# Five arriving-weight slots and nine split-weight slots become four and ten, with a table and four decay rows rehoused

## The chip, the core and the metric

The kernel runs on one core of a Trainium2 chip. The metric is the device time of one execution in microseconds (us): 879.27 us is the median of three runs of the kernel before (878.99 to 879.74).

## What is computed

Two transformer blocks of depth 2 and 1 are run after one another on a sequence of 256 tokens of width 1024, all in fp32. Cut to what matters:

```
for i in range(2):                                   # first_block
    h = x @ w_in[i]
    mix = gated spatial mixer (i = 0)  or  12-head causal attention (i = 1)
    mem_out = 4-head attention of q_mem into 256 memory tokens
    x = layer_norm(ALPHA * x + concat(mix, mem_out) @ w_mix_out[i])
    x = layer_norm(ALPHA * x + (silu(x @ w_g) * (x @ w_u)) @ w_ffn_out[i])     # FFN A, FFN B
mod = silu(c) @ w_ada + b_ada                        # second_block: six rows of 1024
h = rms_norm(x) * (1 + scale1) + shift1
mix = concat(short convolution, 4-head retention with rotary q and k and decay rows) @ w_out
x = x + gate1 * rms_norm(mix)
h = rms_norm(x) * (1 + scale2) + shift2
x = x + gate2 * rms_norm(relu(h @ w_fc1)**2 @ w_fc2)                           # FFN D
```

## The kernel before, in words

**Weights.** All projection weights come from one packed tensor, `w_packed`, in 512 KB pieces (128 partitions by 1024 fp32). A piece is fetched by one DMA of the SP queue into a `raw` slot (L219). Then `split` makes two fp32r tiles of it in an `hl` slot: ScalarE casts the high part (L199), and VectorE subtracts that from `raw` to get the low part (L200). The raw slot is free when the subtraction ends. The hl slot is free when the last matmul that reads it ends. A product then takes three matmuls: high by high, low by high and high by low (`mm_s`, L261; `mm_w2`, L279 and L284; `mm_w`, L269).

**Order.** `weight_plan` lists the chunks in the order of use; an entry has one to four pieces. `chunk(key)` fetches ahead to the entry that is at least LEAD = 6 pieces past the one in use. The tile framework fixes, when the program is built, one order for each engine, by the order of the program, the raised priority of some stretches (`urgent`) and its own estimate of when slots come free; at run time every queue keeps that order. A boundary (`close`, `open_units`) is a layer norm between two stages.

**The slots.** `BUFS` gives five raw and nine hl slots. In the gated FFNs (A and B, 11 pairs of 256 columns) an iteration of the loop over p takes a "g" entry of four pieces (L279 and L284, from both halves of the gate) and an "o" entry of two pieces (L261), for the output of pair p - 2.

**The adaLN rows.** `ada_step` computes `silu(c) @ w_ada` on VectorE (L777, L779) from w_ada pieces of 512 KB, which are loaded into the same raw slots (L774): 32 pieces in FFN A, four after each of the pairs p = 2 to 9, and 16 in FFN B, two after each of p = 2 to 7 and four after p = 8. `ada_end` multiplies the sums with ones on TensorE (L788).

**The small tiles.** `sm(shape, tag)` has a number of slots for each tag, from `SMALL`, otherwise four. The tag `qm` has one slot of 128 by 512 fp32. It holds the memory queries of each layer, and in the retention the decay rows of one head after another (`dec`, L973, loaded at L974 and read at L981). `tab` holds the cosine and sine of the rotary embedding; `rotary_tables` fills it during FFN B (L865 to L885), and `qk_proj` reads it (L967, L968).

Of the kernel before, what the change touches and what calls it, by code (L numbers as in the profile page):

```python
# [10 lines left out]
F32 = mybir.dt.float32  # L11
# [7 lines left out]
P = 128  # L19
S = 256  # L20
D = 1024
# [6 lines left out]
SMALL = {'cg': 2, 'hs': 2, 'sg': 2, 'up': 2, 'qm': 1, 'pr': 4, 'pt': 2}  # L28
LEAD = 6
NS = {'A': 2, 'B': 2, 'D': 4}  # L30
BUFS = {'raw': 5, 'hl': 9, 'ph': 8, 'bc': 4}
FINE = 2
LAG = {'A': 1, 'B': 1, 'D': 2}
WARM = 10
# [98 lines left out]
def model_kernel(  # L133
# [10 lines left out]
    const = ctx.enter_context(tc.tile_pool(name="const", bufs=1))  # L144
    rawp = ctx.enter_context(tc.tile_pool(name="rawp", bufs=BUFS["raw"]))
    hlp = ctx.enter_context(tc.tile_pool(name="hlp", bufs=BUFS["hl"]))
    actp = ctx.enter_context(tc.tile_pool(name="actp", bufs=2))
    bcp = ctx.enter_context(tc.tile_pool(name="bcp", bufs=BUFS["bc"]))
    php = ctx.enter_context(tc.tile_pool(name="php", bufs=BUFS["ph"]))
    smp = ctx.enter_context(tc.tile_pool(name="smp", bufs=2))  # L150
# [5 lines left out]
    def nm(s):  # L156
        uid[0] += 1
        return f"{s}{uid[0]}"

    def bank():  # L160
        return psp.tile([P, 512], F32, tag="ps", name=nm("ps"))
# [2 lines left out]
        return php.tile(shape, dt, tag="ph", name=nm("ph"))  # L164

    def sm(shape, tag, dt=F32):
        return smp.tile(shape, dt, tag=tag, name=nm(tag), bufs=SMALL.get(tag, 4))


    ident = const.tile([P, P], F32, name="ident")  # L170
# [56 lines left out]
    def chunk(key):  # L227
        state["at"] = at_of[key]
        fetch(ahead())
        return ready[key]  # L230


    def urgent():
        return tc.high_priority(offset=URGENT)
# [52 lines left out]
    def joined(dst, o):  # L287

        c = sm([P, S], "cg")
        nc.scalar.copy(c, o[:, S:])  # L290
        return nc.vector.tensor_add(dst, o[:, :S], c)  # L291

    def rstd_of(v0, v1, eps):

        r = sm([P, 1], "rstd")
        nc.vector.tensor_scalar(r, v0, v1, eps, op0=OP.add, op1=OP.add)  # L296
        nc.gpsimd.tensor_tensor(r, r, mhalf, op=OP.pow)  # L297
        return r
# [16 lines left out]
    def layer_norm_act(t, accs, g, b):  # L315

        xx = xt[t]
        s = sm([P, 2], "st")
        for h, cs in enumerate(HALVES):
            nc.vector.scalar_tensor_tensor(xx[:, cs], xx[:, cs], ALPHA, accs[h], op0=OP.mult, op1=OP.add,  # L320
                                           accum_out=s[:, h:h + 1])
        nb = sm([P, 1], "nb")
        nc.vector.tensor_scalar(nb, s[:, 0:1], s[:, 1:2], -1.0 / (32.0 * D), op0=OP.add, op1=OP.mult)
        v = sm([P, 2], "mv")
        junk = bank()
        for h, cs in enumerate(HALVES):
            nc.scalar.activation(junk, xx[:, cs], AF.Square, bias=nb, scale=1.0 / 32.0, accum_out=v[:, h:h + 1])
        nmu = sm([P, 1], "nmu")
        nc.vector.tensor_scalar(nmu, nb, 32.0, None, op0=OP.mult)
        for cs in HALVES:  # L330
            nc.vector.scalar_tensor_tensor(xx[:, cs], xx[:, cs], nmu, g[:, cs], op0=OP.add, op1=OP.mult)
        r = rstd_of(v[:, 0:1], v[:, 1:2], LN_EPS)
        for cs in HALVES:
            nc.vector.scalar_tensor_tensor(xx[:, cs], xx[:, cs], r, b[:, cs], op0=OP.mult, op1=OP.add)
# [324 lines left out]
            nc.vector.bn_stats(st3[t][:, b], vl[t][:, S * b:S * b + S])  # L659

    def v_norm(t):
        mv = sm([P, 2], "mv2")
        nc.vector.bn_aggr(mv, st3[t])
        r = rstd_of(mv[:, 1:2], 0.0, LN_EPS)
        nc.vector.scalar_tensor_tensor(vl[t], vl[t], mv[:, 0:1], lvg, op0=OP.subtract, op1=OP.mult)
        nc.vector.scalar_tensor_tensor(vl[t], vl[t], r, lvb, op0=OP.mult, op1=OP.add)
# [15 lines left out]
    hl = chunk(("Av", 0))  # L682
# [12 lines left out]
    for h in range(2):  # L695
        nc.sync.dma_start(bsb[64 * h:64 * h + 64], bass.AP(
            tensor=a_b_s.tensor, offset=a_b_s.offset + P * h, ap=[[0, 64], [2 * P, 6], [1, P]]))
    v_norm(0)
    v_norm(1)
    ubuf = [ph([P, 3, S]) for _ in range(2)]  # L700
    for j in range(6):
# [30 lines left out]
    qm = sm([P, 2, S], "qm")  # L732
# [94 lines left out]
    qm = sm([P, 2, S], "qm")  # L827
# [28 lines left out]
    close([part(0, 3)], [part(1, 2), part(1, 3)], mixo.acc, bnd)  # L856


    tab = const.tile([P, 2, S], F32, name="tab")
    freq = const.tile([P, 2], F32, name="freq")  # L860

    def rotary_tables():
# [107 lines left out]

    def ret_scores(h):

        dec = sm([P, 384], "qm")  # L973
        nc.sync.dma_start(dec, k_decay[h])  # L974
        q, k = qk_of[h][:, 0], qk_of[h][:, 1]
        ps = bank()
        nc.tensor.matmul(ps[:, :S], k[:, :P], q, start=True, stop=True)
        nc.tensor.matmul(ps[:, S:384], k[:, P:], q[:, P:], start=True, stop=True)
        s_of[h] = sm([P, 384], "pt")
        with urgent():  # L980
            nc.vector.tensor_mul(s_of[h], ps[:, :384], dec)  # L981
# [61 lines left out]
    for h in range(4):  # L1043
        qk_proj(h, 0)
        if h >= 2:
            ret_scores(h - 2)
        qk_proj(h, 1)
        if h >= 2:
            ret_values(h - 2)
    y = conv_in(0)  # L1050
    ret_scores(2)
    conv_out(0, y)
    ret_values(2)
    ret_scores(3)
    y = conv_in(1)
    ret_values(3)
# [105 lines left out]
```

## Time and profile before

| | |
|---|---|
| median of three runs | 879.27 us |
| the profiled execution | 880.1 us, of which its span is 876.9 us |
| TensorE matmul busy | 866.3 us, 99% of the span |
| TensorE weight load busy | 730.0 us, 83% |
| VectorE, ScalarE busy | 650.3 us (74%), 488.1 us (56%) |
| moved by DMA | 195.7 MB, mean 223 GB/s |

The difference of 3.2 us between the execution and its span lies outside the profile's instructions. Matmuls overlap one another in the profile, so the busy share of TensorE shows that it was never left without work for long, not that each matmul ran at its shortest.

### The profile page before, as it was taken

To read this page: it belongs to the slowest core of one execution; us is meant where nothing else is said; L and a number is where in the kernel's file an instruction comes from. 1 tells how busy PE (TensorE), PEld (TensorE's weight loads), DVE (VectorE), ACT (ScalarE), POOL (GpSimd) and SP (SyncE) were. 2 spreads that over 40 slices of the span, in tenths; PEclk is the share of its full clock that TensorE was granted. 3 is DMA by queue.
4 is the path that set the end of the run, shared out by engine and by line. 5 is a ranking of instruction groups with operands and counts; after the bars stand their busy time and mean duration, and the time that the engine had idled before them with its cause. 6 is when DMAs were issued, how large, how long until landed. Compare 5 with 4: busy or idle time off the path is not lost.

```text
span 876.9 us, 12811 instructions
## 1 busy us (share of the span) xinstructions
PE 866.3 (99%) x4678; PEld 730.0 (83%) x4678; DVE 650.3 (74%) x982; ACT 488.1 (56%) x887; POOL 21.5 (2%) x32
## 2 busy tenths in 40 slices
PE   9999999999999999999999999999999999999997
PEld 6888888888887888778888888878988888888885
DVE  6877967888989778767877767797777975555542
ACT  6666454545544567545645644565555676666641
POOL 0100000000000000000000000020010100000000
PEclk9999999999999999999999999999999999999999
DMA  8987757888987763426876777558645566555511
GB/s 317 329 287 228 239 188 253 287 302 308 317 297 258 240 240 121 144 93 200 306 245 230 246 264 266 206 181 290 210 168 195 180 212 213 191 192 191 188 56 48
DMA packets 60355, 195.70 MB, mean 223 GB/s; under 512 B 9209, under 2 KB 12537, under 8 KB 60293
## 3 DMA queue, kind: packets, MB, share of 16 engines
q1 hardware_dynamic: 59860, 194.57, 65.5%
q8 instruction: 36, 0.59, 0.3%
q10 hardware_dynamic: 432, 0.33, 0.1%
q14 instruction: 27, 0.21, 0.1%
HBM read 193.80 MB, written 1.07 MB: 222 GB/s over the span
## 4 chain that ended last, share of the span: by engine, by line
PE 82%; DVE 6%; DMA 5%; issue 3%; ACT 3%; POOL 0%; SPq 0%; POOLq 0%; DVEq 0%; ACTq 0%
PE ps L261 38%; PE ps L279 23%; PE ps L284 12%; DMA raw<-w_ada 4%; DVE hl L200 3%; PE ps L269 3%; ACT hl L199 2%; DMA raw<-w_packed 1%; PE ps L590 1%; PE ps L547 1%; DVE ph L779 1%; PE ps L686 1%; PE ps L244 1%; PE ps L581 1%; POOL rstd L297 0%
## 5 line engine op out<-in xcount | busy, mean ns | idle before, releaser
L200 DVE TENSOR_TENSOR hl<-raw,hl 128x1024 fp32r<-128x1024 f32 (+1 forms) x294 | 348.2, 1204 | 112.7 <-ACT hl L199 112.0
L199 ACT CAST hl<-raw 128x1024 fp32r<-128x1024 f32 (+1 forms) x294 | 296.8, 1039 | 133.3 <-DMA raw<-w_packed 58.0
L261 PE MATMUL ps<-hl,ph 128*128 128x512 f32 x912 | 213.0, 390 | 0.0
L261 PEld LDWEIGHTS ps<-hl,ph 128*128 128x128 f32 x912 | 171.0, 188 | 36.2 <-ACT cg L290 0.8
L279 PE MATMUL ps<-yT,hl 128*128 128x512 f32 x576 | 147.6, 393 | 0.0
L279 PEld LDWEIGHTS ps<-yT,hl 128*128 128x128 f32 x576 | 104.5, 189 | 19.5 <-issue 0.8
L284 PEld LDWEIGHTS ps<-yT,hl 128*128 128x128 f32 x576 | 78.6, 190 | 5.9 <-DVE hl L200 0.3
L284 PE MATMUL ps<-yT,hl 128*128 128x256 f32 x576 | 80.6, 282 | 0.1
L290 ACT COPY cg<-ps 128x256 f32<-128x256 f32 x134 | 48.9, 367 | 51.5 <-PE ps L279 51.3
L261 PE MATMUL ps<-hl,mixT 128*128 128x512 f32 x288 | 70.0, 396 | 0.0
L779 DVE SCALAR_TENSOR_TENSOR ph<-raw,cT,ph 128x1024 f32<-128x1024 f32 x42 | 53.8, 1282 | 19.0 <-DMA raw<-w_ada 18.3
L261 PEld LDWEIGHTS ps<-hl,mixT 128*128 128x128 f32 x288 | 53.0, 188 | 12.9 <-issue 2.2
L279 PE MATMUL ps<-fT,hl 128*128 128x512 f32 x192 | 50.2, 392 | 0.0
L279 PE MATMUL ps<-xT,hl 128*128 128x512 f32 x176 | 46.9, 397 | 0.0
L199 ACT CAST ph<-hs 128x256 fp32r<-128x256 f32 x60 | 24.4, 406 | 38.6 <-DVE hs L452 37.8
L261 PE MATMUL ps<-hl,yT 128*128 128x512 f32 x192 | 45.3, 392 | 0.1
L261 PEld LDWEIGHTS ps<-hl,yT 128*128 128x128 f32 x192 | 35.6, 188 | 8.3 <-ACT yT L249 0.5
L200 DVE TENSOR_TENSOR ph<-hs,ph 128x256 fp32r<-128x256 f32 x60 | 25.3, 422 | 21.4 <-ACT ph L199 20.1
L279 PEld LDWEIGHTS ps<-fT,hl 128*128 128x128 f32 x192 | 35.2, 189 | 6.3
L279 PEld LDWEIGHTS ps<-xT,hl 128*128 128x128 f32 x176 | 31.6, 189 | 6.8 <-issue 1.0
L297 POOL TENSOR_TENSOR rstd<-rstd,mhalf 128x1 f32<-128x1 f32 x18 | 17.1, 949 | 788.8 <-DVE rstd L296 788.8
L450 ACT ACTIVATE sg<-sg 128x256 f32<-128x256 f32 x36 | 15.0, 418 | 30.6 <-DVE sg L291 30.6
(181 smaller groups left out, 932.2 us busy)
## 6 DMA issues: line engine op xcount, KB each, us to landing
raw<-w_packed SPq DMA_DIRECT2D x286, 512.0 KB
raw<-w_ada SPq DMA_DIRECT2D x48, 512.0 KB
bc<-mod SPq DMA_DIRECT2D x6, 512.0 KB
raw<-w_packed SPq DMA_DIRECT2D x8, 256.0 KB
ph<-x_t SPq DMA_DIRECT2D x8, 128.0 KB
ph<-mem_t SPq DMA_DIRECT2D x2, 512.0 KB
xt<-x SPq DMA_DIRECT2D x2, 512.0 KB
bc<-ln_mix_g SPq DMA_DIRECT2D x2, 512.0 KB
```

The lines of the kernel that those rows point to most:

```text
L199: a = nc.scalar.copy(dst_hi, src)
L200: b = nc.vector.tensor_sub(dst_lo, src, dst_hi.bitcast(F32))
L244: nc.tensor.transpose(p4[:, k], src[:, 512 * h + P * k:512 * h + P * (k + 1)], ident)
L261: nc.tensor.matmul(o, aT[:, a, k0 + k, tok], hl(b, k, cols), start=start and n == 0, stop=stop and n == 3 * nk - 1)
L269: nc.tensor.matmul(o, hl(b, k, cols), aT[:, a, k, :], start=n == 0, stop=n == 3 * nk - 1)
L279: nc.tensor.matmul(both, hl(0, k, cols), aT[:, :, k, :], start=k == 0, stop=k == nk - 1)
L284: nc.tensor.matmul(o[:, :S], hl(1, k, cols), aT[:, 0, k, :], start=False, stop=False)
L290: nc.scalar.copy(c, o[:, S:])
L297: nc.gpsimd.tensor_tensor(r, r, mhalf, op=OP.pow)
L450: nc.scalar.activation(g, g, AF.Silu)
L547: nc.tensor.matmul(sps[h][:, o], self.q[hs, qs], self.k[hs, ks], start=True, stop=True)
L779: nc.vector.scalar_tensor_tensor(acc, raw, sc, acc, op0=OP.mult, op1=OP.add)
```

## The change

There is one raw slot less (512 KB) and one hl slot more (1 MB). What pays for it: the small tags without an entry in `SMALL` have two slots instead of four, the norm of `v` uses the tag `mv` instead of one of its own, the rotary table moves from a tile of its own into the `qm` slot, and the decay rows leave `qm` and go through a raw slot, as a weight piece does.

```
-BUFS = {'raw': 5, 'hl': 9, 'ph': 8, 'bc': 4}
+BUFS = {'raw': 4, 'hl': 10, 'ph': 8, 'bc': 4}
...
     def sm(shape, tag, dt=F32):
-        return smp.tile(shape, dt, tag=tag, name=nm(tag), bufs=SMALL.get(tag, 4))
+        return smp.tile(shape, dt, tag=tag, name=nm(tag), bufs=SMALL.get(tag, 2))
...
     def v_norm(t):
-        mv = sm([P, 2], "mv2")
+        mv = sm([P, 2], "mv")
...
-    tab = const.tile([P, 2, S], F32, name="tab")
+    tab = sm([P, 2, S], "qm")
...
     def ret_scores(h):
 
-        dec = sm([P, 384], "qm")
+        dec = rawp.tile([P, D], F32, tag="raw", name=nm("raw"))[:, :384]
         nc.sync.dma_start(dec, k_decay[h])
```

## Rows read from the trace of the kernel before

**Rows 1.** The page: busy us (share of the span) and instructions.

```profile
PE 866.3 (99%) x4678; PEld 730.0 (83%) x4678; DVE 650.3 (74%) x982; ACT 488.1 (56%) x887; POOL 21.5 (2%) x32
```

**Rows 2.** Windows of 20 us, FFN A and D; last: clock, DMA share, GB/s.

```profile
180.00:200.00 20.00, 20.00 (x109) 17.30 (x108) 16.76 (x21) 9.81 (x16) 0.00 (x0) 1.00 0.89 307
...
780.00:800.00 20.00, 20.00 (x105) 17.14 (x104) 10.52 (x15) 12.47 (x23) 0.00 (x0) 1.00 0.63 203
```

**Rows 3.** Waits of TensorE's weight loads: total us, times, longest us.

```profile
PEld ps L686 <- DVE hl L200: 1.3, 3, 0.5
PEld ps L261 <- DVE hl L200: 1.2, 3, 0.6
...
PEld ps L261 <- ACT hl L199: 0.7, 1, 0.7
...
PEld ps L284 <- DVE hl L200: 0.3, 1, 0.3
```

**Rows 4.** The chain that ended last, FFN A: start us, length us.

```profile
154.17 5.46 PE ps L261 x24
159.63 1.59 PE ps L279 x7
...
170.78 5.46 PE ps L261 x24
...
257.82 1.59 PE ps L279 x7
```

**Rows 5.** Timelines of FFN A: start us, length us, instruction, idle time before it.

```profile
154.88 1.23 DVE L200 TENSOR_TENSOR hl<-raw,hl 128x1024 fp32r<-128x1024 f32 x1 [0.85 <-ACT hl L199]
...
159.06 0.33 SPq L219 DMA_DIRECT2D raw<-w_packed  x1
...
159.29 5.24 DVE L779 SCALAR_TENSOR_TENSOR ph<-raw,cT,ph 128x1024 f32<-128x1024 f32 x4
...
163.24 0.33 SPq L219 DMA_DIRECT2D raw<-w_packed  x1
...
164.13 1.05 ACT L199 CAST hl<-raw 128x1024 fp32r<-128x1024 f32 x1 [5.79 <-DMA raw<-w_packed]
...
165.22 1.23 DVE L200 TENSOR_TENSOR hl<-raw,hl 128x1024 fp32r<-128x1024 f32 x1 [0.69 <-ACT hl L199]
...
170.62 5.62 PE L261 MATMUL ps<-hl,ph 128*128 128x512 f32 x24
...
171.34 1.03 ACT L199 CAST hl<-raw 128x1024 fp32r<-128x1024 f32 x1
...
258.18 1.22 DVE L200 TENSOR_TENSOR hl<-raw,hl 128x1024 fp32r<-128x1024 f32 x1 [0.86 <-ACT hl L199]
```

**Rows 6.** The chain that ended last, FFN B.

```profile
453.48 6.16 DMA raw<-w_ada
...
529.06 3.81 DMA raw<-w_ada
```

**Rows 7.** The chain that ended last, boundary after FFN B.

```profile
575.86 1.67 DVE hl L200 x2
...
579.88 0.64 PE ps L244 x4
```

**Rows 8.** Timelines of the retention and the waits between 600 and 668 us.

```profile
642.36 0.56 DVE L981 TENSOR_TENSOR pt<-ps,qm 128x384 f32<-128x384 f32 x1 [0.44 <-DMA qm<-k_decay]
...
644.04 2.00 ACT L199 CAST hl<-raw 128x1024 fp32r<-128x1024 f32 x2 [1.68 <-PE ps L284]
...
ACT hl L199 <- DMA raw<-w_packed: 0.3, 1, 0.3
```

**Rows 9.** Lines L881 and L974: count, durations ns, first and last start.

```profile
L881 ACT ACTIVATE tab<-sg x1: 419/419/419, 441.0 to 441.0; 128x256 f32<-128x256 f32 x1
...
L974 SPq DMA_DIRECT2D qm<-k_decay x4: 328/328/328, 371.9 to 638.5; - x4
```

**Rows 10.** Waits over the whole span, softmax sums of the attention.

```profile
DVE sums L571 <- ACT pr L564: 3.6, 6, 1.0
```

## The prediction

> **What bounds the kernel now.** I read the page first. TensorE's matmuls are busy for 866.3 of 876.9 us [rows 1], and in windows of 20 us they fill the window in FFN A and in FFN D alike, at a granted clock of 1.00, which is the 2.4 GHz level [rows 2]. The windows also tell the stages apart: FFN A takes 307 GB/s from memory and FFN D 203. Busy matmuls can hide stalls, so the next view is the list of what ended the waits of the weight loads. The reader is to see how little of it is the wait for a split weight: the four largest such rows make 1.3 + 1.2 + 0.7 + 0.3 = 3.5 us in the whole execution [rows 3], and the first of them is the start of the kernel (L686). In FFN A the chain of work that ended last holds TensorE alone, and an "o" entry starts each 170.78 - 154.17 = 16.61 us [rows 4]. So TensorE's own stream sets the time, and this change can act only where pieces come late. The place to look is FFN A, where the pieces come fastest.
>
> The Trainium skill (Perfetto Trace Analysis, Identifying the Most-Contended Engine) warns that busy matmuls are no good measure and names the busy share of the weight loads instead. That is 83% here [rows 1], so by this rule some 17% of the span, 147 us, would be room, and a slot more could be worth much. The trace differs: only 3.5 us of that idle time ends with a split weight [rows 3].
>
> **The supply in FFN A.** Each pair needs six weight pieces and four w_ada pieces through the raw slots. The timelines give what a slot costs [rows 5]. A weight piece is issued at 159.06 and its cast begins at 164.13, when ScalarE had been waiting for the DMA: 5.07 us. The subtraction that frees the slot ends at 165.22 + 1.23 = 166.45, so a weight holds a slot for 7.39 us at least. A w_ada piece holds it for the same 5.07 and then 5.24 / 4 = 1.31 us on VectorE, 6.38 us. A pair costs 6 x 7.39 + 4 x 6.38 = 69.9 slot-us. Five slots could serve a pair in 14.0 us, four in 17.5 us, while TensorE takes 16.61.
>
> How it goes with five is to be seen in the lead of the pieces. The last piece of the "g" entry of p = 4 is split at 154.88 + 1.23 = 156.11 [rows 5], and TensorE starts that entry at 159.63 and reads its first low part 1.59 us later [rows 4]: a lead of 5.1 us. For p = 10 the same points are 258.18 + 1.22 = 259.40 [rows 5] and 257.82 + 1.59 = 259.41 [rows 4]: a lead of 0.0. (The last piece's own low part is read six short matmuls later, which I estimate at 0.7 us from the 1.59 us of seven long ones at half their width.) Over these six pairs TensorE took 98.2 us and the pieces 103.3, or 17.2 each. So five slots already fall behind TensorE, and the lead just lasts.
>
> Why 17.2 and not 14.0: arrived pieces sit in raw slots. The fourth piece of the entry is issued at 163.24, is there at about 168.3 by the same 5.07 us, and is cast at 171.34, just after TensorE has left the entry before it at 170.62 [rows 5]. It is the piece for which no split slot was free: four in use, two of "o" and three of the new entry make nine. It held its raw slot for 3.0 us for nothing.
>
> **Part by part.** *Ten hl slots.* The fourth piece fits, so those 3.0 us go, from the raw slot's time and from the readiness of the whole entry. Elsewhere the slot can take away at most the waits of [rows 3] without the start, 1.2 + 0.7 + 0.3 = 2.2 us. I take 0.3, the wait at L284, since it is that of the last, fourth piece of an entry late in FFN B.
>
> *Four raw slots.* Outside FFN A the supply holds. With two w_ada pieces a pair FFN B needs (6 x 7.39 + 2 x 6.38) / 4 = 14.3 us of the 16.61. In FFN D four slots bring 4 x 0.524 MB / 7.39 us = 284 GB/s, against the 203 that it takes [rows 2]. There a raw slot less and an hl slot more leave fourteen places, and the pieces ahead stay as many. In FFN A the time per pair lies between two bounds. With the shortest DMA that the chain shows, 3.81 us [rows 6], it is (69.9 - 10 x 1.26) / 4 = 14.3, less than TensorE's. If every wait of today but the 3.0 us stayed, it is (17.2 x 5 - 3.0) / 4 = 20.8; the longest DMA, 6.16 [rows 6], gives nearly as much, 20.2. I take 17.5, from the DMA of FFN A itself, since four slots have no more pieces in flight than five, and their later issue eats most of the waiting behind other pieces. Six pairs then take 105.0 us against 98.2, so 6.8 us of lead are used; there are 5.1 + 0.7 + 3.0 = 8.8. Nothing reaches TensorE, but only by 2.0 us.
>
> The Trainium skill (DMA: Bandwidth & Descriptors, Anatomy of one DMA — SWDGE (gpsimd) path) gives a transfer about 2.0 us and its bytes at 436 GB/s, which for 512 KB is 3.2 us, on another queue than SP's. By it a pair would cost (69.9 - 10 x 1.87) / 4 = 12.8 us and four slots would never bind. This trace differs in FFN A, with 5.07 us [rows 5], and comes nearer only at 3.81 [rows 6].
>
> *Decay rows through a raw slot.* Four DMAs of 192 KB take a raw slot each, and SP issues them among the weights as before. One was late by 0.44 us for VectorE at 642.36, and no piece of weight is: between 600 and 668 us ScalarE waits for a weight's DMA for 0.3 us in all, and the casts begin when TensorE frees a split slot (1.68 us before the one at 644.04) [rows 8]. A decay row kept in a raw slot until L981 therefore takes space from pieces that wait anyway. Price 0; without that cover at most one weight's slot time, 7.39 us, late once, and the lead there is not read from a row. The lower bound is a gain of 0.4.
>
> *The table in qm.* The decay row was loaded into `qm` from 371.9 on, so the slot was free by then, and the table is first written at 441.0 [rows 9]. Price 0 with 69 us of cover.
>
> *Two small slots for four.* Softmax sums of two heads fill both slots, so the next pair's exponentials wait for the normalising of this one. That is ordered before them on VectorE already, and it waits for ScalarE 3.6 us in six times [rows 10]. If each wait doubled and TensorE felt it, 3.6 us; I take 0, since the query and key products beside the causal pairs cover it.
>
> **The sum.** 880.1 us of the profiled execution (span 876.9, outside it 3.2) - 0.3 + 0 = 879.8. The profiled execution is 0.8 over the median, so the runs should show 879.0.
>
> **Rivals.** *The ring of four stalls TensorE at the end of FFN A (slower).* Place: the "g" entries from p = 7 to 10. It decides from (98.2 + 8.8) / 6 = 17.8 us a pair, against the 17.5 taken. At 18.5 the six pairs take 111.0, so 4.0 us reach TensorE: 883. At the bound of 20.8 it is 124.8 - 107.0 = 17.8 us, 897. For it: five slots ran 3.2 us over their own minimum. Against it: part of that is the wait for the split slot.
>
> *The order of splits changes at a boundary (either way).* After FFN B two splits, 1.67 us, stand in the chain in front of the transposes at 579.88 [rows 7]. Pieces that are split earlier leave the chain; one piece more in it costs half of that, 0.8 us. At one boundary neither end is measured as a change; at three with a split more, 2.5 us, 881.5.
>
> *The tenth slot takes all the waits for split weights after the start (faster).* 2.2 us under the median: 877.1. For it: they are waits for just that. Against it: three of them are short of a piece or of VectorE, not of a slot.
>
> **Chances.** A measurement of this kernel tells 0.2%, 1.8 us, from no change. Forecast, within that: 0.47. Ring: 0.28, its margin being small. Splits late at several boundaries: 0.07. Faster by the slot, or by it and splits that leave a boundary: 0.18. So faster 0.18, same 0.47, slower 0.35. The likeliest case alone spans 877.5 to 881. The range takes in most of the ring's stalls and of the gain: 876.8 to 885.
>
> **What would show it.** In FFN A the fourth piece's cast should begin before TensorE leaves the entry before it, and the "g" entries should be split at intervals of about 17.5 us, with a lead that ends between 0 and 3 us. If weight loads at L279 or L284 wait for L199 or L200 between 200 and 262 us, the ring has bound. In FFN B the wait of 0.3 us at L284 should be gone. The decay rows should be issued earlier and L981 should not wait. Wrong it would be if FFN A's pairs took over 16.61 us, or if a boundary grew by more than 2 us.

## The result, and the profile after

The changed kernel takes 890.13 us (median of six runs, 887.31 to 893.93) against 879.13 us for the kernel before on the same chip. The ratio is 1.0125, 95% interval 1.0108 to 1.0142: 11.0 us slower, where the forecast was 879.0. The profiled execution of the changed kernel took 893.9 us, with a span of 892.0. That is the slowest of its six runs, so the 15.1 us by which its span exceeds the one of before (876.9) is more than the 11.0 us of the medians; the places are read from it, the sizes with that in mind.

The page of the changed kernel: its busy line, and its chain of work that ended last, by line. The busy line answers to [rows 1].

```profile
PE 872.1 (98%) x4678; PEld 731.9 (82%) x4678; DVE 651.2 (73%) x982; ACT 489.7 (55%) x887; POOL 21.0 (2%) x32
...
PE ps L261 31%; PE ps L279 15%; DMA raw<-w_packed 10%; PE ps L284 8%; DVE hl L200 6%; ACT hl L199 4%; DMA raw<-w_ada 4%; PE ps L269 3%; DVE ph L779 1%; PE ps L590 1%; PE ps L686 1%; PE ps L244 1%; DVE hs L291 1%; PE ps L547 1%; DVE hs L452 1%
```

The same chain by line in the kernel before:

```profile
PE ps L261 38%; PE ps L279 23%; PE ps L284 12%; DMA raw<-w_ada 4%; DVE hl L200 3%; PE ps L269 3%; ACT hl L199 2%; DMA raw<-w_packed 1%; PE ps L590 1%; PE ps L547 1%; DVE ph L779 1%; PE ps L686 1%; PE ps L244 1%; PE ps L581 1%; POOL rstd L297 0%
```

No engine does more work: the counts of instructions are those of [rows 1], and VectorE's and ScalarE's busy times are within 2 us of them. (TensorE is busy for 5.8 us more with the same matmuls, some of which ran at its lower clock, as the last section shows.) But the transfer of a weight is now 10% of the chain, where it was 1%. In FFN A of before, the chain held TensorE alone [rows 4]; here it runs through the loads. The chain of the changed kernel in FFN A, start and length in us:

```profile
161.25 5.51 DMA raw<-w_packed
...
174.02 6.37 DMA raw<-w_ada
...
197.93 5.66 DMA raw<-w_packed
...
256.31 4.72 DMA raw<-w_packed
```

The windows of the changed kernel: most of FFN A, the two windows that answer to [rows 2], and four short ones at the end of FFN A. The columns are the busy us (and instructions) of PE, PEld, DVE, ACT and POOL, then granted clock, DMA share and GB/s.

```profile
140.00:250.00 110.00, 110.00 (x585) 93.92 (x584) 88.72 (x110) 51.66 (x84) 0.00 (x0) 1.00 0.85 286
...
180.00:200.00 20.00, 20.00 (x108) 17.30 (x107) 16.64 (x20) 8.61 (x14) 0.00 (x0) 1.00 0.84 280
780.00:800.00 20.00, 20.00 (x105) 17.12 (x104) 11.24 (x15) 13.06 (x22) 0.00 (x0) 1.00 0.59 192
...
258.00:262.00 4.00, 1.96 (x7) 0.78 (x5) 2.79 (x3) 3.03 (x5) 0.00 (x0) 1.00 0.95 309
262.30:265.50 3.20, 3.04 (x10) 2.23 (x11) 3.20 (x6) 3.04 (x5) 0.00 (x0) 0.50 0.88 285
266.00:270.00 4.00, 4.00 (x23) 3.44 (x22) 3.92 (x6) 1.69 (x3) 0.00 (x0) 1.00 0.87 316
...
286.20:289.30 3.10, 3.10 (x8) 2.35 (x8) 2.86 (x5) 0.00 (x0) 0.00 (x0) 0.50 0.82 287
```

TensorE is full between 140 and 250 us, but memory brings 286 GB/s, and between 180 and 200 us 280 where it brought 307 [rows 2]. A pair moves ten pieces of 0.524 MB in the 16.61 us that TensorE takes, which needs 316 GB/s. The lead is being spent, and no busy share shows it. Then, between 258 and 262 us, TensorE is busy for half the time.

The timeline of TensorE in the changed kernel, from the last "o" entry ahead of g(10) to the boundary after FFN A, and from g(10) of FFN B to the boundary after it:

```profile
255.73 2.90 PE L261 MATMUL ps<-hl,ph 128*128 128x512 f32 x12
258.50 0.73 PE L279 MATMUL ps<-yT,hl 128*128 128x512 f32 x2
260.15 0.73 PE L279 MATMUL ps<-yT,hl 128*128 128x512 f32 x2 [0.92 <-ACT hl L199]
262.15 1.12 PE L279 MATMUL ps<-yT,hl 128*128 128x512 f32 x2 [1.27 <-ACT hl L199]
263.43 0.79 PE L279 MATMUL ps<-yT,hl 128*128 128x512 f32 x1 [0.16 <-ACT hl L199]
264.02 1.87 PE L284 MATMUL ps<-yT,hl 128*128 128x256 f32 x8
...
267.57 1.11 PE L284 MATMUL ps<-yT,hl 128*128 128x256 f32 x8
...
277.18 1.06 PE L788 MATMUL ps<-ph,ones 128*32 128x512 f32 x8
...
282.68 0.49 PE L261 MATMUL ps<-hl,ph 128*128 128x512 f32 x1 [0.76 <-DVE hl L200]
284.91 12.68 PE L261 MATMUL ps<-hl,ph 128*128 128x512 f32 x46 [1.74 <-ACT ph L199]
297.43 1.03 PE L244 MATMUL ps<-ident,xt 128*128 128x128 f32 x8
...
561.08 1.89 PE L279 MATMUL ps<-yT,hl 128*128 128x512 f32 x7 [0.93 <-DVE sg L291]
...
579.38 13.80 PE L261 MATMUL ps<-hl,ph 128*128 128x512 f32 x58 [0.93 <-ACT ph L199]
...
595.06 1.29 PE L244 MATMUL ps<-ident,ph 128*128 128x128 f32 x8 [1.88 <-DVE ph L924]
```

The four landmarks in the kernel before, and the start of g(10) of FFN B: the output entry ahead of g(10), the row of L788 that follows g(10) and one more output entry, and the transposes of L244 after FFN A and after FFN B.

```profile
254.91 2.90 PE L261 MATMUL ps<-hl,ph 128*128 128x512 f32 x12
...
271.64 1.06 PE L788 MATMUL ps<-ph,ones 128*32 128x512 f32 x8
...
286.65 1.03 PE L244 MATMUL ps<-ident,xt 128*128 128x128 f32 x8
...
548.13 1.76 PE L279 MATMUL ps<-yT,hl 128*128 128x512 f32 x7
...
579.88 1.29 PE L244 MATMUL ps<-ident,ph 128*128 128x128 f32 x8 [1.07 <-DVE ph L924]
```

So the changed kernel is 0.8 us late at the first landmark, 5.5 at the second, 10.8 at the third, 15.2 at the fourth, and 15.1 at the end. The loss stands at three places: 4.7 us in g(10), where the second, third and fourth piece of the entry are awaited; 5.2 us in the last output entries, which SP issues behind the four w_ada pieces of pair 9; and 4.4 us between the two boundaries. There TensorE is 11.9 us late at g(9) of FFN B, 12.9 at g(10), 14.4 at the end of the outputs and 15.2 at the transposes, before which its idle time grew from 1.07 to 1.88 us. The first 1.1 us of this third place are lost ahead of g(3) of FFN B. They are not the w_ada pieces': ada_bc, few_in_B and few_in_A_and_B below lose them too, raw5_hl9 does not, and their cause stays open. The table of the experiments uses the four landmarks.

### The profile page after: what moved, and what is told of

The parts are those of the page before. It is cut to its first block, busy times and chain, and to the rows that moved or that the text cites. A ratio compares the mean times of both kernels' runs of the same rounds, so it can differ in the third digit from the quotient of the medians.

```text
span 892.0 us, 12810 instructions
## 1 busy us (share of the span) xinstructions
PE 872.1 (98%) x4678; PEld 731.9 (82%) x4678; DVE 651.2 (73%) x982; ACT 489.7 (55%) x887; POOL 21.0 (2%) x32
## 3 DMA queue, kind: packets, MB, share of 16 engines
HBM read 193.80 MB, written 1.07 MB: 218 GB/s over the span
## 4 chain that ended last, share of the span: by engine, by line
PE 63%; DMA 13%; DVE 11%; ACT 6%; issue 6%; POOL 0%; SPq 0%; POOLq 0%; DVEq 0%; ACTq 0%
PE ps L261 31%; PE ps L279 15%; DMA raw<-w_packed 10%; PE ps L284 8%; DVE hl L200 6%; ACT hl L199 4%; DMA raw<-w_ada 4%; PE ps L269 3%; DVE ph L779 1%; PE ps L590 1%; PE ps L686 1%; PE ps L244 1%; DVE hs L291 1%; PE ps L547 1%; DVE hs L452 1%
## 5 line engine op out<-in xcount | busy, mean ns | idle before, releaser
L261 PE MATMUL ps<-hl,ph 128*128 128x512 f32 x912 | 216.1, 393 | 3.8 <-ACT ph L199 2.7
L279 PE MATMUL ps<-yT,hl 128*128 128x512 f32 x576 | 149.4, 395 | 3.3 <-ACT hl L199 2.3
L284 PEld LDWEIGHTS ps<-yT,hl 128*128 128x128 f32 x576 | 79.5, 192 | 5.8
L284 PE MATMUL ps<-yT,hl 128*128 128x256 f32 x576 | 81.2, 284 | 0.0
L199 ACT CAST ph<-hs 128x256 fp32r<-128x256 f32 x60 | 24.4, 407 | 49.3 <-DVE hs L452 48.4
L297 POOL TENSOR_TENSOR rstd<-rstd,mhalf 128x1 f32<-128x1 f32 x18 | 16.9, 938 | 804.7 <-DVE rstd L296 804.7
```

The lines of the kernel that those rows point to most:

```text
L199: a = nc.scalar.copy(dst_hi, src)
L261: nc.tensor.matmul(o, aT[:, a, k0 + k, tok], hl(b, k, cols), start=start and n == 0, stop=stop and n == 3 * nk - 1)
L279: nc.tensor.matmul(both, hl(0, k, cols), aT[:, :, k, :], start=k == 0, stop=k == nk - 1)
L284: nc.tensor.matmul(o[:, :S], hl(1, k, cols), aT[:, 0, k, :], start=False, stop=False)
```

## The experiments

**Theory A (the ring):** with four raw slots the pieces of a pair take longer than TensorE's 16.61 us wherever four w_ada pieces go with six weight pieces. **Theory B (the rest):** the table in `qm`, the decay rows, the two small slots or the moved order cost the time. The table gives what each run's TensorE stream lost against the kernel before between one landmark and the next (us, start of the same row of the timelines, rounded; the last column is the difference of the spans). It is read from the profiled executions, which took 2.5 to 4.0 us more than the medians in the changed kernel, ada_3of4, ada_2of4, no_tail and few_in_B, so a difference of a microsecond between two rows is not read. "Until g(10)" ends at the output entry ahead of it.

| run | until g(10) | g(10) | to end of FFN A | to after FFN B | rest | all |
|---|---|---|---|---|---|---|
| changed kernel | 0.8 | 4.7 | 5.2 | 4.4 | -0.1 | 15.1 |
| raw4_hl9 | 3.1 | 5.0 | 2.1 | 6.0 | 0.7 | 16.9 |
| ada_bc | -0.5 | 0.0 | -0.3 | 0.8 | -0.4 | -0.3 |
| raw3_hl10_ada_bc | 6.3 | 0.0 | -0.3 | 4.5 | 3.1 | 13.6 |
| ada_3of4 | 4.6 | 0.2 | 6.1 | 5.6 | 1.2 | 17.7 |
| ada_2of4 | 2.0 | 0.0 | 1.4 | 5.1 | 1.2 | 9.8 |
| no_tail | -0.3 | 3.6 | -0.3 | 4.4 | 1.3 | 8.8 |
| few_in_B | 0.2 | 5.1 | 5.8 | 0.8 | -0.5 | 11.3 |
| few_in_A_and_B | -0.2 | 0.0 | -0.3 | 0.8 | -0.3 | 0.0 |

**raw5_hl9** keeps every other edit and takes back the two sizes.

```diff
-BUFS = {'raw': 4, 'hl': 10, 'ph': 8, 'bc': 4}
+BUFS = {'raw': 5, 'hl': 9, 'ph': 8, 'bc': 4}
```

> All edits of the change but the slots: five raw and nine hl slots stay. If the ring of four raw slots costs the time (theory A), this is the kernel before within 1.8 us: 877.5 to 881. If the small tags with two slots, the table in qm or the decay rows in a raw slot cost it (theory B), it is near the changed kernel: 888 or more.

Measured: 879.24 us, ratio 0.9997 (0.9987 to 1.0007). Theory B falls: the table, the decay rows and the small slots together cost nothing.

**raw4_hl9** is the changed kernel without the tenth split slot (`'raw': 4, 'hl': 9`).

> The changed kernel with nine hl slots in place of ten, so that the raw slot is lost and nothing is won. Theory A: the pieces of a pair in FFN A take 18.3 us as in the changed kernel or more, since the fourth piece of an entry waits for a split slot again, up to 3.0 / 4 = 0.75 us a pair; over eight pairs 0 to 6 us on top of the 890, so 890 to 896. Theory C, that the tenth hl slot itself costs the time, because casts that may start earlier stand in front of other work on ScalarE: 878 to 882.

Measured: 894.38 us, 1.0167 (1.0147 to 1.0188). The loss is the missing raw slot's, and the tenth split slot, with four raw slots, is a gain of about 4 us (894.38 - 890.13).

**ada_bc** is the changed kernel with the w_ada pieces taken out of the ring, into the four slots of the tag `bc`; **before_ada_bc** is the same edit in the kernel before.

```diff
-            raw = rawp.tile([P, D], F32, tag="raw", name=nm("raw"))
+            raw = bcp.tile([P, D], F32, tag="bc", name=nm("bc"))
```

> The changed kernel, with the w_ada pieces in the bc slots, which stand empty in the middle of both FFNs; the raw slots hold weights and decay rows alone. Theory A: a pair needs 6 x 7.39 / 4 = 11.1 us of the four raw slots, less than the 16.61 of TensorE, so the 9.9 us of FFN A and most of the 3 us at the end of FFN B come back: 878 to 882. Theories B and C: 888 or more.

> The kernel before, with the same move of the w_ada pieces into the bc slots. Theory A: TensorE waited for no piece in FFN A, so nothing comes back: 877.5 to 880.5. If the lead that falls to 0.0 us there costs something already, up to 2 us less: 877.

Measured: ada_bc 879.65 us, 1.0005 (0.9996 to 1.0015); before_ada_bc 878.76 us, 0.9996 (0.9986 to 1.0005). All of the loss comes back with the same bytes over the same queue, so it is the count of slots and not memory's rate as such. Every edit can also change the orders that the framework fixes for the engines, and no run holds these still; but raw5_hl9, ada_bc and few_in_A_and_B bring the time back by three different edits. The window of ada_bc:

```profile
140.00:250.00 110.00, 110.00 (x585) 93.96 (x584) 99.43 (x123) 57.28 (x91) 0.00 (x0) 1.00 0.89 319
```

It brings 319 GB/s where the four shared slots brought 286 and TensorE needs 316. In the kernel before the edit is worth nothing: five slots were just enough.

**raw3_hl10** goes one slot further (`'raw': 3, 'hl': 10`), and **raw3_hl10_ada_bc** adds the edit of ada_bc to it.

> The changed kernel with three raw slots. The ring as measured: in FFN A of the changed kernel a weight held its slot for 7.74 us and a w_ada piece for 6.67 on the mean, 73.1 slot-us a pair, 18.3 us with four slots and 24.4 with three. From p = 4 to p = 10 that is 146 us against the 98.2 of TensorE less 8.8 of lead, so 39 us late there, 5 more for the last output pieces, and in FFN B (6 x 7.74 + 2 x 6.67) / 3 = 19.9 us a pair against 16.61, over seven pairs some 14 us after the lead: near 935, range 915 to 950. Rival: a piece lands sooner with fewer in flight (3.81 us as in the shortest case), 57.3 / 3 = 19.1 us a pair in FFN A: 890 to 900.

> Three raw slots and the w_ada pieces in the bc slots. The ring: six weights a pair, 6 x 7.74 / 3 = 15.5 us, less than 16.61, so three slots carry both FFNs: 878 to 884. If the number of raw slots costs by something other than their time per pair: more than 890.

Measured: raw3_hl10 935.69 us, 1.0634 (1.0610 to 1.0658), as expected, but not by the expected sum. The last pieces of its g(4) and g(10) in FFN A were split at

```profile
162.14 1.23 DVE L200 TENSOR_TENSOR hl<-raw,hl 128x1024 fp32r<-128x1024 f32 x1 [0.88 <-ACT hl L199]
...
290.71 1.23 DVE L200 TENSOR_TENSOR hl<-raw,hl 128x1024 fp32r<-128x1024 f32 x1 [1.40 <-ACT hl L199]
```

so the six pairs took 128.6 us, 21.4 each, and not the 24.4 that came from the stays of the changed kernel: with three slots a weight piece stayed for 6.55 us where it had stayed for 7.74. TensorE lost 20.8 us from g(4) to g(10) where 39 were expected, and nothing from g(3) to g(10) of FFN B where 14 were. The rest of the loss stands ahead of these stretches and behind them, so that the total came out as expected is luck.

raw3_hl10_ada_bc took 893.01 us, 1.0156 (1.0139 to 1.0172), a miss. In FFN A it lost nothing, as the ring says, but 6.3 us were gone before it, and the 4.5 between FFN A and the end of FFN B were gone before g(3) of FFN B. The waits of TensorE's weight loads in raw3_hl10_ada_bc between 60 and 115 us, in the first mixing stage:

```profile
PEld ps L590 <- ACT pt L583: 2.2, 1, 2.2
PEld ps L261 <- ACT mixT L199: 1.3, 1, 1.3
PEld ps L261 <- DVE mixT L200: 0.8, 1, 0.8
```

They are waits for the softmax and for the mixed rows, not for a weight. So three slots cost time outside the pairs, where the sum per pair does not look. Whether the cause is ScalarE's order, in which these stand among casts of pieces that are late, was not tried.

**ada_moved** moves eight steps (16 pieces) of w_ada from FFN A into FFN B, which leaves two pieces a pair in A.

```diff
-... hook=spread(16, 0, NS["A"], NPAIR - 1))
+... hook=spread(8, 0, NS["A"], NPAIR - 1))
...
-    spread_b = spread(8, 16, NS["B"], NPAIR - 2, True)
+    spread_b = spread(16, 8, NS["B"], NPAIR - 2, True)
```

> The changed kernel with the second third of the w_ada pieces moved from FFN A to FFN B: two a pair in FFN A, 4.6 in FFN B. The ring: FFN A (6 x 7.74 + 2 x 6.67) / 4 = 14.9 us a pair, no loss; FFN B (6 x 7.74 + 4.6 x 6.67) / 4 = 19.3 against 16.61, over seven pairs 19 us less a lead of 8.8, so some 10 us lost, after 500 us of the span: 887 to 893. If the loss belonged to FFN A as a place: 879 to 882.

Measured: 896.57 us, 1.0200 (1.0177 to 1.0222). The place is right: its transposes after FFN A start at 286.33 us, 0.3 earlier than before, and those after FFN B at 596.23, 16.4 later. The size is off by 4 to 10 us. The 16 steps, spread over seven pairs of FFN B, put four pieces after five of them and six after two; by the stays read below (7.74 and 6.67 us) those take 5 x 18.3 + 2 x 21.6 = 134.7 us against 7 x 16.61 = 116.3, so 18.4 us less whatever lead there was, an estimate made after the run. In FFN B, between 500 and 565 us, its weight loads waited 10.4 us for casts:

```profile
PEld ps L279 <- ACT hl L199: 10.4, 9, 2.6
```

**ada_3of4** leaves out every fourth w_ada piece in FFN A (that part of the product is not computed), and **ada_2of4** every second one.

```diff
-        for k in range(2):
+        for k in range(1 if rnd < 2 and i % 2 else 2):
...
-        for k in range(2):
+        for k in range(1 if rnd < 2 else 2):
```

> The changed kernel without every fourth w_ada piece of FFN A (its product is left out), three a pair in place of four. The ring: (6 x 7.74 + 3 x 6.67) / 4 = 16.6 us a pair, as long as TensorE takes, so the 9.9 us of FFN A go and the 3.6 of the end of FFN B stay: 879 to 883. If the loss grew in proportion to the pieces: 890 - 10 / 4 = 887 or more.

> The changed kernel with two w_ada pieces after each of the pairs 2 to 9 of FFN A where it has four; the other half of that part of the product silu(c) @ w_ada is left out. By the slot times measured in the changed kernel (7.74 us for a weight piece, 6.67 for a w_ada piece) a pair takes (6 x 7.74 + 2 x 6.67) / 4 = 15.0 us, well under TensorE's 16.61; with three of four it was 16.6, no margin at all, and the time was 893.9. Theory (the ring binds where its time per pair reaches TensorE's): FFN A loses nothing at p = 10 and at most half of the 5.2 us at the last output entries, and the 3.6 us at the end of FFN B stay: 879 + 3.6 + 0 to 2.6 = 882 to 885.5. Rival (taking pieces out of FFN A mends nothing, since the order of the splits moves and a stall comes up elsewhere, as with three of four): 888 to 894.

Measured: ada_3of4 893.93 us, 1.0154 (1.0130 to 1.0179), a miss, with a time above the changed kernel's that its rival does not explain either; ada_2of4 885.07 us, 1.0058 (1.0032 to 1.0085), at the upper end of what was expected. Both lose next to nothing in g(10), but not because a pair took the 16.6 and 15.0 us that were worked out. By the last splits of g(4) and g(10) it took 18.0 in ada_3of4 (153.03 to 260.83) and 17.6 in ada_2of4 (150.52 to 255.91): with fewer w_ada pieces the weight pieces stayed longer, 8.74 and 9.53 us. What saved g(10) is the lead at g(4), 8.7 and 10.7 us where the changed kernel had 6.5. And ada_3of4 lost 4.6 us ahead of g(10). Its timelines of VectorE and TensorE there, and a window of 3 us:

```profile
219.99 1.22 DVE L200 TENSOR_TENSOR hl<-raw,hl 128x1024 fp32r<-128x1024 f32 x1 [0.83 <-ACT hl L199]
221.13 0.68 DVE L794 TENSOR_TENSOR pr<-pr,ps 128x512 f32<-128x512 f32 x1
...
221.87 3.36 PE L279 MATMUL ps<-yT,hl 128*128 128x512 f32 x7 [2.12 <-DVE pr L794]
...
222.00:225.00 3.00, 3.00 (x7) 2.38 (x8) 2.51 (x3) 1.65 (x4) 0.00 (x0) 0.50 0.40 127
```

The sum of `ada_end` (L794) stands on VectorE behind the subtraction of a piece that came late, and TensorE waited 2.12 us for that sum, after which its clock stood at 0.50 for these 3 us. In ada_2of4 the same wait took 1.5 us. So a late piece also stalls TensorE by what is queued behind its split. In the changed kernel L794 stands between w_ada products instead, and nothing waits for it.

**no_tail** leaves out the four w_ada pieces after pair 9. **few_in_B** leaves 4 of the 16 w_ada pieces in FFN B. **few_in_A_and_B** leaves out both of these and every second piece in FFN A. What is left out is that part of the product.

```diff
-        for k in range(2):
+        for k in range(0 if i in (14, 15) else 2):
...
-        for k in range(2):
+        for k in range(2 if rnd < 2 or kc == 0 else 0):
...
-        for k in range(2):
+        for k in range(0 if i in (14, 15) else 1 if rnd < 2 else 2 * (kc == 0)):
```

> The changed kernel without the four w_ada pieces that are loaded after pair 9, the last four of FFN A; that part of the product silu(c) @ w_ada is left out. In the changed kernel TensorE's stream loses 5.2 us between 270 and 285 us, where the last output entries of FFN A start, and SP issues these entries behind those four pieces; it loses 4.6 us before that, at the g entry of p = 10, whose pieces are issued ahead of them. Theory (each loss comes from what stands ahead in the ring of four slots): the 5.2 us go, the 4.6 us at p = 10 and the 3.6 us at the end of FFN B stay: 890.1 - 5.2 = 885, between 884 and 886.5. Rival (the ring's loss goes with the number of pieces, wherever they stand): 4 of 48 w_ada pieces are 8 per cent of the loss of 11 us, 889 to 890.

> The changed kernel with 4 w_ada pieces in FFN B where it has 16 (the first two of each of the two products), FFN A unchanged; the rest of that part of the product silu(c) @ w_ada is left out. Theory (the 3.6 us that TensorE's stream loses between 540 and 585 us, at the end of FFN B, come from the four w_ada pieces after p = 8 in the ring of four slots): they go, and FFN A's loss stays: 886 to 887. Rival (the order of splits at the boundary after FFN B, not the ring): nothing changes there, 889.5 to 891.

> The three omissions together: two w_ada pieces after each of the pairs 2 to 8 of FFN A, none after pair 9, and four in all of FFN B; the rest of the product silu(c) @ w_ada is left out. Theory (all of the change's loss is the ring of four slots, with the w_ada pieces in it): no loss in FFN A nor at the end of FFN B, what is left are the 1.0 us in the attention and the 0.9 us at the start of FFN B: 879 to 881. Rival (the four slots lose somewhere whatever the w_ada pieces do): 884 or more.

Measured: no_tail 885.24 us, 1.0067 (1.0048 to 1.0086); few_in_B 887.61 us, 1.0086 (1.0058 to 1.0113); few_in_A_and_B 879.49 us, 0.9991 (0.9979 to 1.0003). Each takes away the loss of its own place and leaves the others: no_tail turns 5.2 us into -0.3 and keeps 3.6 at g(10); few_in_B turns 4.4 into 0.8 (ada_bc has this 0.8 too) and keeps 5.1 and 5.8 in FFN A; together nothing is left. few_in_B leaves out pieces after the pairs 3, 4, 5 and 7 of FFN B too, not only the four after pair 8, so its 3.6 us (2.5 by the medians) are those of all twelve. The median of few_in_B is 0.6 us over its expected range, which its interval covers. The landmarks of few_in_A_and_B, to be held against the same three rows of before above:

```profile
271.42 1.06 PE L788 MATMUL ps<-ph,ones 128*32 128x512 f32 x8
...
286.15 1.03 PE L244 MATMUL ps<-ident,xt 128*128 128x128 f32 x8
...
580.16 1.29 PE L244 MATMUL ps<-ident,ph 128*128 128x128 f32 x8 [1.07 <-DVE ph L924]
```

No run beat the kernel before by more than a measurement can tell.

## Why the prediction was wrong

**The bound was read rightly.** Little time was to be won: before_ada_bc, which gives the kernel before more slots than either version, changed nothing.

**The step that failed is the ring's term, "I take 17.5".** Over the same six pairs, the last piece of g(4) and of g(10) were split in the changed kernel at

```profile
154.01 1.23 DVE L200 TENSOR_TENSOR hl<-raw,hl 128x1024 fp32r<-128x1024 f32 x1
...
263.61 1.22 DVE L200 TENSOR_TENSOR hl<-raw,hl 128x1024 fp32r<-128x1024 f32 x1
```

which ends at 155.24 and 264.83: 109.6 us, 18.3 a pair. The prediction's own threshold was 17.8, and it left a margin of "only 2.0 us" on one instance of a load. The 36 weight pieces issued from 141.9 to 251.7 us hold their slot for 7.74 us on average (5.35 from the issue to the cast, 2.39 to the end of the subtraction), and the 24 w_ada pieces for 6.67 (5.45 and 1.22): (6 x 7.74 + 4 x 6.67) / 4 = 18.3, the interval just read. In the kernel before they held it for 8.82 and 7.90, or 84.5 / 5 = 16.9 a pair; so a slot less did shorten the stay, as the prediction expected, but to 7.74 and 6.67 and not to the 7.39 and 6.38 that were taken. (In a ring that is always full, such an agreement follows from the counting, whatever makes the stays long. That the slots are the cause is shown by ada_bc and few_in_A_and_B.) The 7.39 came from the first piece of a batch [rows 5], for which ScalarE was idle. From issue to use the mean weight piece takes 0.3 us more than that one, the mean w_ada piece 0.4.

**The margin was smaller, too.** The 3.0 us of the fourth piece were counted whole into the lead. The fourth piece of g(5) is cast 5.5 us after its issue in the changed kernel (166.16 to 171.69) where [rows 5] has 7.8 (both from the end of the issue), so the slot was there. But g(4) was ready only 155.24 against 156.11, 0.9 us earlier, and TensorE was late by 0.7 itself. With its first low part at 161.73 the lead was 6.5 us where 8.1 was counted. Then 109.6 - 98.2 = 11.4 us were used of 6.5 + 0.7 = 7.2, so 4.2 should reach TensorE at g(10), and 4.7 did. Nor did five slots fall behind by 17.2 against 16.61 in every pair, as the prediction's average has it. In the kernel before the lead at g(9) was still 4.5 us (split by 240.85, first low part at 245.35), of the 5.1 at g(4); the rest went in the last pair, whose output entry is half as long (2.90 us at 254.91). With four slots 7.2 us had gone by g(9).

**The rival was right in its mechanism and too small.** "4.0 us reach TensorE: 883" priced g(10) alone, and came near its 4.7 us because two errors cancel: it had a pair at 18.5 us where 18.3 was measured, and a lead of 8.8 where 7.2 was there. It had left out that the last output entries stand behind the four w_ada pieces of pair 9 (5.2 us, shown by no_tail).

**"Outside FFN A the supply holds" failed in FFN B.** The 14.3 us a pair were worked out with the same short stays and with two w_ada pieces, the mean; after p = 8 there are four. The last pieces of g(3), g(9) and g(10) of FFN B were split in the changed kernel at

```profile
435.01 1.22 DVE L200 TENSOR_TENSOR hl<-raw,hl 128x1024 fp32r<-128x1024 f32 x1
...
539.57 1.23 DVE L200 TENSOR_TENSOR hl<-raw,hl 128x1024 fp32r<-128x1024 f32 x1 [0.73 <-ACT hl L199]
...
560.94 1.22 DVE L200 TENSOR_TENSOR hl<-raw,hl 128x1024 fp32r<-128x1024 f32 x1
```

From g(3) to g(9) a pair took 17.4 us, with two w_ada pieces in most of them, and the lead fell from 11.8 to 6.9 us; the last pair, behind four, took 21.4, and its lead was gone. few_in_B shows the twelve pieces that it leaves out to cost 3.6 us, and in FFN D, where there are none, nothing was lost.

**What held.** The price 0 of the table, the decay rows and the small slots (raw5_hl9). The last decay row is now issued at 648.7, 7.9 us ahead of its use, where it was issued 3.9 us ahead (638.5 in [rows 9], 642.36 in [rows 8]), and L981 waits no more. The loads of L974 and the last L981 in the changed kernel:

```profile
L974 SPq DMA_DIRECT2D raw<-k_decay x4: 327/328/328, 626.6 to 648.7; - x4
...
656.63 0.56 DVE L981 TENSOR_TENSOR pt<-ps,raw 128x384 f32<-128x384 f32 x1
```

The wait of 0.3 us at L284 [rows 3] is gone as well: no row of the changed kernel has it. The tenth slot is worth more than the 0.3 us taken, about 4 us, in a kernel that the missing raw slot has made late; with five raw slots it was not tried.

**Right by luck.** The rival of the boundaries priced a split more at 0.8 us, and after FFN B the wait did grow by 1.88 - 1.07 = 0.8 us. But no split was added. Two splits stand ahead of the transposes before and after, and what came late are VectorE's additions to `xt` (L320). Before:

```profile
567.97 0.69 DVE L320 SCALAR_TENSOR_TENSOR xt<-xt,ps 128x512 f32<-128x512 f32 x1 [0.67 <-PE ps L261]
...
575.78 2.35 DVE L200 TENSOR_TENSOR hl<-raw,hl 128x1024 fp32r<-128x1024 f32 x2
```

In the changed kernel:

```profile
583.16 0.68 DVE L320 SCALAR_TENSOR_TENSOR xt<-xt,ps 128x512 f32<-128x512 f32 x1
...
590.96 2.35 DVE L200 TENSOR_TENSOR hl<-raw,hl 128x1024 fp32r<-128x1024 f32 x2
```

Before, VectorE stood ready and waited for TensorE's sum; in the changed kernel it came to L320 straight from late splits. From the second addition to the transposes it is 11.9 us in both. In few_in_B the waits of 0.67 and 1.07 us are back. Whether the 0.8 us until g(10), lost for the most part before FFN A's pairs, belong to the change stays open: no_tail and few_in_A_and_B don't have them.

## What to carry to other kernels

A ring of buffers is sized by (sum over an iteration of each load's stay, from issue to release) / slots against the iteration's time. But the stay is not a property of the load: that of a weight piece, over six pairs of FFN A, was 8.82 us with five slots (and nine split slots), 7.74 with four, 6.55 with three, and 9.53 with four and half the w_ada pieces. So an uncrowded load gives only the lower end, the mean stay of one ring is an estimate for another (24.4 us a pair for 21.4, 15.0 for 17.6), and a margin of a few per cent is none. In a trace, read how the lead of the pieces changes from one iteration to the next. Work it out for the worst stretch, not for the stage's mean, and for what is issued behind the last burst. Before giving a slot of such a ring to another use, see whether a second kind of load can leave the ring: here the w_ada pieces in idle slots took back the whole loss.

## What the hardware showed

**A load's time fell less than the slots did.** In FFN A the mean from issue to use was 6.32 us (weights) with five shared slots and 5.35 with four, 15% less time for 20% fewer slots; so the rate fell, in the window of 180 to 200 us from 307 to 280 GB/s. With three slots it was 4.22. The Trainium skill (DMA: Bandwidth & Descriptors, Anatomy of one DMA — SWDGE (gpsimd) path) splits the time of a transfer on the GpSimd queue into a fixed part and its bytes at full rate, an estimated 3.2 us for 512 KB. The measured 5.35 us, on SP's queue, is longer; it also holds the wait for ScalarE, and it falls with the number of loads that can be under way.

**A short wait cost TensorE its clock.** After TensorE had been busy for 1.96 of the 4.00 us from 258 on, still at 1.00, the granted clock was 0.50 from 262.3 to 265.5, which is the 1.2 GHz level. TensorE was busy for 3.04 of these 3.20 us, and from 266 on it was back at 1.00. Eight matmuls of L284 took 1.87 us from 264.02 on, 1.11 at the full clock. The same is seen from 286.2 to 289.3, at 0.50, after idle times of 0.76 and 1.74 us, and in ada_3of4 after one of 2.12; around the 1.5 us in ada_2of4 the clock was 1.00, from 216 to 225 us. By the two rows an estimated 1.5 + 1.6 = 3.1 us of work were lost to the clock in FFN A (half of the busy time), a third of its 9.9 us. The Trainium skill (TensorE: Matmul & The Clock Gate, HAM oscillation — how this bites in real kernels) states that a matmul stretch that follows a wait for a transfer can begin at the slower clock, and this trace agrees.
